# A two-layer encoder kernel on one core: PSUM tiles read by one engine after the other, a negated maximum, scaled memory keys and one copy per Fourier block

## The chip, the core and the metric

The kernel runs on one core of a Trainium2 chip. TensorE (PE in the profile, its weight loads PEld) multiplies, VectorE (DVE) and ScalarE (ACT) read its results from PSUM and prepare the next operands, GpSimd (POOL) does elementwise work between SBUF tiles, and DMA queues, most of them issued by SyncE (SP), bring data from HBM. Each engine works through its own instructions in a fixed order and waits where another engine has not delivered yet. The metric is the device time of one execution in microseconds (us); lower is better.

## What is computed

The reference is an encoder of two layers on 1024 tokens of width 1024, in float32. Cut to what matters:

```python
for l in range(2):
    h = rmsnorm(x, g_pre_mix[l])
    zf, zq, zk, zv, zm = split(h @ w_in[l])          # 256, 512, 128, 128, 256 columns
    y_f = real(fftn(zf, over tokens and channels)) @ w_fourier[l]
    y_a = window_attention(rope(zq), rope(zk), zv, sink[l])      # 8 query heads, 2 key heads, +-128 tokens
    km, vm = split(rmsnorm(mem, g_mem[l]) @ w_mem_kv[l])         # 256 memory rows, 4 heads of 64
    scores = zm @ km.T * 64 ** -0.5
    y_m = softmax(scores) @ vm
    y = concat(rmsnorm(y_f), rmsnorm(y_a), rmsnorm(y_m)) @ w_out[l]
    x = x + rmsnorm(y, g_post_mix[l])
    gate, up = split(rmsnorm(x, g_pre_ffn[l]) @ w_ffn_in[l])
    x = x + rmsnorm((silu(gate) * up) @ w_ffn_out[l], g_post_ffn[l])
```

## The kernel before

**Products.** A float32 product is made of three TensorE products in a rounded format: each operand is split in a high part (ScalarE rounds it by a copy) and a low part (VectorE or GpSimd subtracts the high part from the original), and high x high, high x low and low x high are added up in PSUM (`Acc.add`, L185 to L188). So a result that leaves PSUM and is an operand again is read twice: once by ScalarE for the high part and once by VectorE for the low part.

**Stages of a layer.** The first half of a layer mixes tokens, the second half is the feed-forward network. In the mixing half the kernel goes through: the Fourier columns (`zf`, PSUM tile `zT`), then keys, values and memory queries (`kvz`, tile `kvp`) woven with the Fourier units (`fourier_units`, tiles `yfp` and `yfT`), then the queries (`q`, tile `qp`, L187) woven with the eight memory units (`mem_units`: tile `ms`, L900, for scores, `mpT`, L922, for turned probabilities, `mav`, L932, for values), then window attention of one key head (`att_units(0)`: `sc`, L787, `pT`, L824, `av`, L839) woven with output products (`mo`, L187), then attention of the other key head woven with the second output products, the residual and the first products of the feed-forward network. The feed-forward network (`qc`, `qx`, `qy`, `qz`, L1181, then `fo`, L1330) is long rows of 128x512 products.

**What is touched.** Four helpers read a PSUM tile with both engines, in halves of 64 partitions. `q_stack` (L429) is called twice for one tile, once for each half j: ScalarE copies half j (L433), VectorE then subtracts (L434). Its tiles are `zT` (L730, turned memory queries) and `qT` (L767, turned queries). `dup_stack` (L420) does the same with two copies (L424, L425) and two subtractions (L426, L427) per half; its sources are the PSUM tile `kT` (L736, turned keys) and, in `Memory.load`, the memory keys in SBUF. `fourier_tables` splits `abp` (L529 to L533) half by half, and `fold` (L854) adds the two 64-partition parts of `av`. Between two engines that read the same PSUM tile the kernel carries a wait, in the order in which the code is written, so the second half's ScalarE copy stands behind the first half's VectorE subtraction. `mem_scores` (L889) takes the maximum of two 128x256 score blocks (L902), multiplies it by -1/8 on VectorE (L903) and gives it to the exponentials on ScalarE (L906) as their bias. `Memory.keys` copies the keys out of PSUM (L478). `turned` in the Fourier units copies a turned block out of PSUM with two copies (L610), one for each half of the tokens.

**What sets the order.** The code is traced unit by unit, and a list scheduler at build time then chooses each engine's order from the dependencies, the order of the code and its own estimate of durations. So an edit in one helper can move instructions of other units on all engines. PSUM is held in four pools of two banks each (`sc`, `pT`, `av`, `pd`): a tile that is read late keeps its bank from the next tile of its pool. `qT`, `kT`, `av`, `mav` and the small `ssp` share the pool `av`; `zT` of `kvz_turn`, `yfT`, `mpT` and `abp` share `pT`; `ms`, `sc` and `yfp` share `sc`.

## Time and profile before

| What | Value |
|---|---|
| Time, median of 3 runs (lowest, highest) | 2046.52 us (2045.35, 2047.14) |
| The profiled execution's own time | 2045.68 us |
| Its span, first to last instruction | 2043.9 us |
| DVE, ACT, POOL busy | 1499.5, 1047.9, 691.9 us |
| Mixing half of layer 0, about | 50 to 400 us of the span |
| Mixing half of layer 1, about | 1050 to 1400 us |

The profile comes from one execution; 1.8 us of its time lie outside its span, and it is 0.84 us below the median of the runs. The page names an instruction by its line in the kernel, its engine and its operation, with the tile it writes and those it reads. Idle time of an engine is put down to whatever ended it: `PE ms L900 <- ACT flex L425` means that TensorE stood idle until ScalarE's copy of line 425 was done.

### The profile page before, as it was taken

To read this page: it belongs to the slowest core of one execution; us is meant where nothing else is said; L and a number is where in the kernel's file an instruction comes from. 1 tells how busy PE (TensorE), PEld (TensorE's weight loads), DVE (VectorE), ACT (ScalarE), POOL (GpSimd) and SP (SyncE) were. 2 spreads that over 40 slices of the span, in tenths; PEclk is the share of its full clock that TensorE was granted. 3 is DMA by queue.
4 is the path that set the end of the run, shared out by engine and by line. 5 is a ranking of instruction groups with operands and counts; after the bars stand their busy time and mean duration, and the time that the engine had idled before them with its cause. 6 is when DMAs were issued, how large, how long until landed. Compare 5 with 4: busy or idle time off the path is not lost.

```text
span 2043.9 us, 28334 instructions
## 1 busy us (share of the span) xinstructions
PE 1990.0 (97%) x9587; PEld 1630.4 (80%) x9587; DVE 1499.5 (73%) x2378; ACT 1047.9 (51%) x2220; POOL 691.9 (34%) x811
## 2 busy tenths in 40 slices
PE   7999999999999999999999999999999999999998
PEld 6877777778888888887878768777788888887886
DVE  5566767897867766777956667578887777778776
ACT  7476767643333434554545667676333333346441
POOL 4354445224434332002523544451333433410011
PEclk8999999999999999999999999999999999999999
DMA  6111223433333225979731113243343323269883
GB/s 221 53 57 40 95 99 114 145 129 108 107 110 119 81 90 161 315 262 319 265 127 50 47 47 114 84 145 105 127 135 109 102 99 108 85 229 345 304 276 120
DMA packets 181889, 288.56 MB, mean 141 GB/s; under 512 B 15560, under 2 KB 81648, under 8 KB 181744
## 3 DMA queue, kind: packets, MB, share of 16 engines
q1 hardware_dynamic: 173680, 267.88, 39.2%
q10 hardware_dynamic: 8064, 18.88, 2.4%
q8 instruction: 75, 1.23, 0.2%
q14 instruction: 70, 0.57, 0.1%
HBM read 220.11 MB, written 66.58 MB: 140 GB/s over the span
## 4 chain that ended last, share of the span: by engine, by line
PE 84%; DVE 5%; DMA 3%; ACT 3%; POOL 2%; issue 2%; SPq 0%; DVEq 0%; POOLq 0%; ACTq 0%
PE fo L1330 17%; PE qy L1181 11%; PE qx L1181 11%; PE qc L1181 11%; PE mo L187 7%; PE qz L1181 6%; PE qp L187 4%; PE kvp L187 4%; PE zT L187 2%; PE sc L787 2%; PE pT L824 2%; PE qa L1181 1%; PE mav L932 1%; PE av L832 1%; PE av L839 1%
## 5 line engine op out<-in xcount | busy, mean ns | idle before, releaser
L1330 PE MATMUL fo<-arena_r 128*128 128x512 f32 x1512 | 357.2, 393 | 7.7 <-ACT arena_r L176 3.8
L1330 PEld LDWEIGHTS fo<-arena_r 128*128 128x128 f32 x1512 | 285.2, 189 | 69.0 <-ACT arena_r L176 4.7
L176 ACT CAST arena_r<-arena_f 128x512 fp32r<-128x512 f32 (+2 forms) x344 | 185.5, 571 | 181.9 <-DMA arena_f<-actd 76.1
L177 DVE TENSOR_TENSOR arena_r<-arena_f,arena_r 128x512 fp32r<-128x512 f32 x262 | 182.7, 729 | 52.5 <-ACT arena_r L176 43.2
L1181 PE MATMUL qc<-arena_r,flex 128*128 128x512 f32 x912 | 220.5, 390 | 0.0
L1171 ACT CAST flex<-arena_f 128x512 fp32r<-128x512 f32 x148 | 91.9, 621 | 225.6 <-PE qy L1181 66.4
L1181 PEld LDWEIGHTS qc<-arena_r,flex 128*128 128x128 f32 x912 | 171.0, 188 | 36.8
L1181 PE MATMUL qy<-arena_r,flex 128*128 128x512 f32 x576 | 139.9, 390 | 0.0
L1171 ACT CAST arena_r<-arena_f 128x512 fp32r<-128x512 f32 x92 | 57.1, 621 | 160.7 <-DVE arena_f L1168 71.1
L1172 DVE TENSOR_TENSOR flex<-arena_f,flex 128x512 fp32r<-128x512 f32 x148 | 112.7, 762 | 27.4 <-ACT flex L1171 27.3
L1215 POOL TENSOR_TENSOR arena_f<-arena_f 128x512 f32<-128x512 f32 x36 | 48.3, 1342 | 231.8 <-ACT arena_f L1186 231.8
L1181 PEld LDWEIGHTS qy<-arena_r,flex 128*128 128x128 f32 x576 | 107.8, 188 | 23.1 <-DVE arena_r L177 0.4
L1181 PE MATMUL qx<-arena_r 128*128 128x512 f32 x360 | 119.3, 389 | 0.0
L1181 PE MATMUL qy<-arena_r 128*128 128x512 f32 x480 | 116.1, 389 | 0.0
L1172 DVE TENSOR_TENSOR arena_r<-arena_f,arena_r 128x512 fp32r<-128x512 f32 x92 | 68.2, 741 | 61.5 <-ACT arena_r L1171 61.2
L1181 PE MATMUL qz<-arena_r,flex 128*128 128x512 f32 x320 | 106.5, 395 | 0.0
L1181 PEld LDWEIGHTS qy<-arena_r 128*128 128x128 f32 x480 | 90.1, 188 | 18.7
L1168 DVE TENSOR_TENSOR arena_f<-arena_f 128x512 f32<-128x512 f32 x90 | 97.3, 1085 | 7.3 <-DMA arena_f<-in_w_ffn_in 5.6
L1222 POOL TENSOR_TENSOR arena_f<-arena_f 128x512 f32<-128x512 f32 x36 | 60.0, 1667 | 124.5 <-DVE arena_f L1221 124.5
L235 POOL TENSOR_SCALAR rrsv<-rss 128x1 f32<-128x1 f32 x32 | 14.8, 463 | 257.3 <-ACT arena_f L350 195.8
L1242 POOL TENSOR_TENSOR arena_f<-arena_f,flex 128x512 f32<-128x512 f32 x32 | 54.4, 1701 | 137.8 <-DVE arena_f L1218 53.8
L177 POOL TENSOR_TENSOR arena_r<-arena_f,arena_r 128x256 fp32r<-128x256 f32 (+2 forms) x82 | 67.6, 829 | 98.1 <-ACT arena_r L176 74.1
(316 smaller groups left out, 4777.0 us busy)
## 6 DMA issues: line engine op xcount, KB each, us to landing
arena_f<-in_w_ffn_out SPq DMA_DIRECT2D x264, 256.0 KB, 4.7
actd<-arena_f SPq DMA_DIRECT2D x154, 256.0 KB, 2.7
arena_f<-actd SPq DMA_DIRECT2D x154, 256.0 KB, 4.6
arena_f<-in_w_ffn_in SPq DMA_DIRECT2D x46, 512.0 KB, 3.8
big<-in_w_ffn_in SPq DMA_DIRECT2D x40, 512.0 KB, 4.5
arena_f<-in_w_in SPq DMA_DIRECT2D x40, 256.0 KB, 2.9
arena_f<-in_x SPq DMA_DIRECT2D x16, 512.0 KB, 4.4
arena_f<-in_w_out SPq DMA_DIRECT2D x32, 256.0 KB, 2.7
```

Source lines behind the costliest of these rows:

```text
L176: nc.scalar.copy(hi, src)
L177: return (lo_eng or nc.vector).tensor_tensor(out=lo, in0=src, in1=f32(hi), op=ALU.subtract)
L187: mm(self.dst, a, b, start=self.i == 0, stop=self.i == self.n - 1)
L787: mm(pt, lhs, self.kst[g][i][:, k0 * P : k1 * P], start=i == 0, stop=i == 1)
L1168: nc.vector.tensor_tensor(out=s, in0=x, in1=y, op=op)
L1171: self.cast = nc.scalar.copy(w[:, 0], s)
L1172: nc.vector.tensor_tensor(out=w[:, 1], in0=s, in1=f32(w[:, 0]), op=ALU.subtract)
L1181: mm(pt, a, b, start=start and n == 0, stop=n == 11, skip_group_check=not start)
L1215: G(out=self.u2, in0=self.u2, in1=self.p1, op=ALU.add)
L1222: G(out=self.p5, in0=self.p1, in1=self.p5, op=ALU.add)
L1242: (G if i % 2 else V).tensor_tensor(out=a[i], in0=c, in1=g[i], op=ALU.mult)
L1330: mm(pt, ab[:, 0, x, sl], ab[:, 1, y], start=new and first and j == 0, stop=last and j == 2, skip_group_check=not new)
```

## The change

The reads of a PSUM tile are written engine by engine: `q_stacks` and `dup_stacks` take both halves of a tile, write all ScalarE copies and then all VectorE subtractions; `fourier_tables` and `fold` do the same. `mem_scores` lets the reduction itself negate the maximum and drops the multiplication; the factor 1/8 moves into the copy of the memory keys, and the exponentials lose their scale. `turned` makes one copy of 128x256 in place of two of 128x128. No product is added or taken away: TensorE has the same instructions. Over the whole program VectorE has 32 instructions fewer (the multiplications) and ScalarE 16 fewer (the copies). In the changed kernel the lines are shifted by some numbers: L433 is L435, L610 is L614, L900 is L901, L732 is L736.

```diff
@@ -417,21 +417,25 @@
             acc.add(hsl(hT, half, 0, k, sl), hsl(hT, half, 1, k, sl), w[k][0], w[k][1])
 
 
-    def dup_stack(kh, kl, src, j):
-
-        r = slice(64 * j, 64 * j + 64)
-        o = slice(64 - 64 * j, 128 - 64 * j)
-        nc.scalar.copy(kh[r], src[r])
-        nc.scalar.copy(kh[o], src[r])
-        nc.vector.tensor_tensor(out=kl[r], in0=src[r], in1=f32(kh[r]), op=ALU.subtract)
-        nc.vector.tensor_tensor(out=kl[o], in0=src[r], in1=f32(kh[r]), op=ALU.subtract)
-
-    def q_stack(dst, src, j):
-
-        r = slice(64 * j, 64 * j + 64)
-        o = slice(64 - 64 * j, 128 - 64 * j)
-        nc.scalar.copy(dst[r], src[r])
-        nc.vector.tensor_tensor(out=dst[o], in0=src[r], in1=f32(dst[r]), op=ALU.subtract)
+    def dup_stacks(dsts, src):
+
+        for j, (kh, kl) in enumerate(dsts):
+            r, o = slice(64 * j, 64 * j + 64), slice(64 - 64 * j, 128 - 64 * j)
+            nc.scalar.copy(kh[r], src[r])
+            nc.scalar.copy(kh[o], src[r])
+        for j, (kh, kl) in enumerate(dsts):
+            r, o = slice(64 * j, 64 * j + 64), slice(64 - 64 * j, 128 - 64 * j)
+            nc.vector.tensor_tensor(out=kl[r], in0=src[r], in1=f32(kh[r]), op=ALU.subtract)
+            nc.vector.tensor_tensor(out=kl[o], in0=src[r], in1=f32(kh[r]), op=ALU.subtract)
+
+    def q_stacks(dsts, src):
+
+        for j, dst in enumerate(dsts):
+            r = slice(64 * j, 64 * j + 64)
+            nc.scalar.copy(dst[r], src[r])
+        for j, dst in enumerate(dsts):
+            r, o = slice(64 * j, 64 * j + 64), slice(64 - 64 * j, 128 - 64 * j)
+            nc.vector.tensor_tensor(out=dst[o], in0=src[r], in1=f32(dst[r]), op=ALU.subtract)
 
 
     class Memory:
@@ -475,7 +479,7 @@
             acc = Acc(pt, NK)
             for k in range(NK):
                 acc.add(self.wk[ci][k][0], self.wk[ci][k][1], self.m(0, k), self.m(1, k))
-            nc.scalar.copy(at(self.ks + ci, NMEM), pt)
+            nc.scalar.activation(at(self.ks + ci, NMEM), pt, AF.Copy, scale=QK_SCALE)
 
         def values(self, mt):
             pt = ps([MW], "vmp", self.tag)
@@ -505,8 +509,7 @@
             km = shaped(reflex(F32R), (2, 2, 2, NMEM))
             self.km = [km[:, i] for i in range(2)]
             for ci in range(2):
-                for j in range(2):
-                    dup_stack(self.km[ci][:, j, 0], self.km[ci][:, j, 1], raw[:, ci], j)
+                dup_stacks([(self.km[ci][:, j, 0], self.km[ci][:, j, 1]) for j in range(2)], raw[:, ci])
 
 
     class Mix:
@@ -528,9 +531,11 @@
                 for s in range(2):
                     pt = ps([HD], "abp", "pT")
                     mm(pt, cc[:, s, :], wf, start=True, stop=True)
-                    for j in range(2):
-                        r = slice(64 * j, 64 * j + 64)
-                        split(AB[r, pr, 0, s, j, :], AB[r, pr, 1, s, j, :], pt[r])
+                    rs = [slice(64 * j, 64 * j + 64) for j in range(2)]
+                    for j, r in enumerate(rs):
+                        nc.scalar.copy(AB[r, pr, 0, s, j, :], pt[r])
+                    for j, r in enumerate(rs):
+                        nc.vector.tensor_tensor(out=AB[r, pr, 1, s, j, :], in0=pt[r], in1=f32(AB[r, pr, 0, s, j, :]), op=ALU.subtract)
             self.AB = AB
             self.PQ = {}
 
@@ -586,7 +591,7 @@
                 TT(E[0], A[0], A[1], ALU.add)
                 TT(E[1], A[0], A[1], ALU.subtract)
                 yf = at(48, 2, 2, 512)
-                self.yf = [yf[:, i] for i in range(2)]
+                self.yf, self.yfs = [yf[:, i] for i in range(2)], yf
 
             def products(r):
                 th, tl, dh, dl = st.pop(("d", r))
@@ -606,11 +611,10 @@
                 pT = ps([2, P], "yfT", "pT")
                 for i in range(2):
                     nc.tensor.transpose(pT[:, i, :], y[:, i * P : (i + 1) * P], ident)
-                for half in range(2):
-                    nc.scalar.copy(
-                        self.yf[half].rearrange("p k (c r) -> p k c r", r=8)[:, :, :, r],
-                        pT[:, :, half * 64 : half * 64 + 64],
-                    )
+                nc.scalar.copy(
+                    self.yfs.rearrange("p h k (c r) -> p h k c r", r=8)[:, :, :, :, r],
+                    pT.rearrange("p k (h c) -> p h k c", h=2),
+                )
 
             def halves(r, dst):
                 raw = raws(2, P)
@@ -730,16 +734,14 @@
             zt = ps([2, P], "zT", "pT")
             for pr in range(2):
                 nc.tensor.transpose(zt[:, pr, :], z[:, pr * P : pr * P + P], ident)
-            for j in range(2):
-                q_stack(self.zst[half][j][:, :, c * P : c * P + P], zt, j)
+            q_stacks([self.zst[half][j][:, :, c * P : c * P + P] for j in range(2)], zt)
             if c == 0:
                 self.kt = ps([4, P], "kT", "av")
             nc.tensor.transpose(self.kt[:, c, :], kr.rearrange("p h d -> p (h d)"), ident)
             if c == 3:
                 ktf = self.kt.rearrange("p c t -> p (c t)")
                 sl = slice(half * 512, half * 512 + 512)
-                for g in range(2):
-                    dup_stack(self.kst[g][0][:, sl], self.kst[g][1][:, sl], ktf, g)
+                dup_stacks([(self.kst[g][0][:, sl], self.kst[g][1][:, sl]) for g in range(2)], ktf)
 
         def skewed(self, f, g, n):
 
@@ -769,8 +771,7 @@
                 nc.tensor.transpose(qt[:, pr, :], qr[:, pr * P : pr * P + P], ident)
             if c == 0:
                 self.qst[half] = [at((64, 0)[half] + 8 * i, 4, 512, dt=F32R) for i in range(2)]
-            for j in range(2):
-                q_stack(self.qst[half][j][:, :, c * P : c * P + P], qt, j)
+            q_stacks([self.qst[half][j][:, :, c * P : c * P + P] for j in range(2)], qt)
 
 
         def att_scores(self, g, n):
@@ -855,10 +856,11 @@
 
             cut = lambda ap: ap.rearrange("p (h s q) -> p s h q", s=2, q=P)
             avh, avl = cut(av[0:64]), cut(av[64:128])
+            d = [dst[64 * s : 64 * s + 64] for s in range(2)]
             for s in range(2):
-                d = dst[64 * s : 64 * s + 64]
-                nc.scalar.copy(d, avl[:, s])
-                nc.vector.tensor_tensor(out=d, in0=avh[:, s], in1=d, op=ALU.add)
+                nc.scalar.copy(d[s], avl[:, s])
+            for s in range(2):
+                nc.vector.tensor_tensor(out=d[s], in0=avh[:, s], in1=d[s], op=ALU.add)
 
         def att_units(self, g):
 
@@ -888,7 +890,6 @@
 
         def mem_scores(self, h, half):
             e = [ems(2, NMEM) for _ in range(2)]
-            rmax = sm(4, "rmax")
             nmx = sm(4, "nmx")
             den = sm(4, "den")
             for b in range(2):
@@ -899,12 +900,11 @@
                     for i in range(2):
                         mm(pt[:, j], lhs, self.mem.km[h // 2][:, h % 2, i], start=i == 0, stop=i == 1)
                 bs = slice(2 * b, 2 * b + 2)
-                nc.vector.tensor_reduce(out=rmax[:, bs], in_=pt, axis=AX.X, op=ALU.max)
-                nc.vector.tensor_scalar_mul(nmx[:, bs], rmax[:, bs], -QK_SCALE)
+                nc.vector.tensor_reduce(out=nmx[:, bs], in_=pt, axis=AX.X, op=ALU.max, negate=True)
                 for j in range(2):
                     c = 2 * b + j
                     nc.scalar.activation(
-                        e[b][:, j], pt[:, j], AF.Exp, bias=nmx[:, c : c + 1], scale=QK_SCALE, accum_out=den[:, c : c + 1]
+                        e[b][:, j], pt[:, j], AF.Exp, bias=nmx[:, c : c + 1], accum_out=den[:, c : c + 1]
                     )
             rden = sm(4, "rden")
             nc.vector.reciprocal(rden, den)
```

The scheduler makes a new order of all engines in the mixing halves; in the long rows of the feed-forward network hardly anything moves. Three places follow, without the numbers of the rows.

The first place is ScalarE at the end of the key stage of layer 0, where the last turned keys (`kT`) and memory queries (`zT`) are stacked; what each instruction waits for stands in brackets. Before:

```order
L424 CAST arena_r<-kT_1168 64x512 [waits PE_49]
L425 CAST arena_r<-kT_1168 64x512
L424 CAST arena_r<-kT_1168 64x512 [waits DVE_49]
L425 CAST arena_r<-kT_1168 64x512
L610 COPY arena_f<-yfT_1371 128x128 [waits PE_49]
L610 COPY arena_f<-yfT_1371 128x128
L433 CAST flex_92<-zT_1376 64x2x128 [waits PE_49]
```

After:

```order
L424 CAST arena_r<-kT_1165 64x512 [waits PE_49]
L425 CAST arena_r<-kT_1165 64x512
L424 CAST arena_r<-kT_1165 64x512
L425 CAST arena_r<-kT_1165 64x512
L614 COPY arena_f<-yfT_1365 128x256 [waits PE_49]
L435 CAST flex_92<-zT_1369 64x2x128 [waits PE_49]
L435 CAST flex_92<-zT_1369 64x2x128
```

The third copy of `kT` no longer waits for VectorE, each Fourier block has one copy, and both copies of `zT` stand in a row; before, the second one stood eight copies of the memory keys later.

TensorE at the same place goes from the first query products (`qp`) to the first memory scores (`ms`). Before:

```order
L187 MATMUL qp_1397<-big_1349,arena_r 128x512 x2
L187 MATMUL qp_1493<-big_1349,arena_r 128x512 x2
L900 MATMUL ms_1466<-flex_1437,arena_r 128x256
L900 MATMUL ms_1475<-flex_1437,arena_r 128x256
L900 MATMUL ms_1466<-flex_1437,arena_r 128x256 x3
L900 MATMUL ms_1475<-flex_1437,arena_r 128x256 x3
```

After:

```order
L187 MATMUL qp_1389<-big_1343,arena_r 128x512 x2
L187 MATMUL qp_1479<-big_1343,arena_r 128x512 x2
L901 MATMUL ms_1454<-flex_1429,arena_r 128x256
L901 MATMUL ms_1462<-flex_1429,arena_r 128x256
L187 MATMUL qp_1556<-big_1319,arena_r 128x512 x6
L187 MATMUL qp_1556<-big_1327,arena_r 128x512 x6
L187 MATMUL qp_1556<-big_1335,arena_r 128x512 x6
L187 MATMUL qp_1556<-big_1343,arena_r 128x512 x3
L901 MATMUL ms_1454<-flex_1429,arena_r 128x256 x3
L901 MATMUL ms_1462<-flex_1429,arena_r 128x256 x3
```

The first two score products need the high part of the memory keys, the third needs the low part; 21 query products now stand between them.

The second place is TensorE at the start of the query products of layer 1. `big_9724` and `big_9732` (`big_9686` and `big_9694` after) hold the weights of the first and second, and of the third and fourth, 128 input rows; of each row block three products are made. Before:

```order
L187 MATMUL qp_9796<-big_9724,arena_r 128x512 x3
L732 MATMUL zT_9625<-const,arena_f 128x128 x2
L187 MATMUL qp_9796<-big_9724,arena_r 128x512 x3
L187 MATMUL qp_9796<-big_9732,arena_r 128x512 x6
L187 MATMUL qp_9796<-big_9740,arena_r 128x512 x3
L608 MATMUL yfT_9654<-const,flex_2276 128x128 x2
L732 MATMUL zT_9690<-const,arena_f 128x128 x2
L187 MATMUL yfp_9705<-arena_r 128x256 x6
```

After:

```order
L187 MATMUL qp_9756<-big_9686,arena_r 128x512 x5
L736 MATMUL zT_9589<-const,arena_f 128x128 x2
L187 MATMUL qp_9756<-big_9694,arena_r 128x512 x3
L187 MATMUL qp_9831<-big_9686,arena_r 128x512 x6
L187 MATMUL qp_9831<-big_9694,arena_r 128x512 x3
L740 MATMUL kT_9532<-const,arena_f 128x128
L187 MATMUL qp_9756<-big_9694,arena_r 128x512
L187 MATMUL qp_9831<-big_9694,arena_r 128x512
L613 MATMUL yfT_9618<-const,flex_2244 128x128 x2
L736 MATMUL zT_9653<-const,arena_f 128x128 x2
L187 MATMUL yfp_9668<-arena_r 128x256 x6
L187 MATMUL qp_9756<-big_9694,arena_r 128x512 x2
```

One product of `qp_9756` more has moved ahead of these rows. The low part of the fourth row block is first needed by the 11th query product before, and by the 21st after; a second token tile (`qp_9831`), six Fourier products and four transposes now stand ahead of it.

The third place is TensorE at the end of the query products of layer 1. Before:

```order
L187 MATMUL qp_10366<-big_9748,arena_r 128x512 x2
L187 MATMUL qp_10366<-big_9748,flex_4658 128x512
L932 MATMUL mav_10268<-arena_f 64x512 x3
L900 MATMUL ms_10244<-flex_9830,flex_4102 128x256 x4
L900 MATMUL ms_10253<-flex_9830,flex_4102 128x256 x4
```

After:

```order
L187 MATMUL qp_10305<-big_9702,flex_4626 128x512
L901 MATMUL ms_10271<-flex_9790,flex_4070 128x256 x4
L187 MATMUL qp_10305<-big_9710,arena_r 128x512 x2
L187 MATMUL qp_10305<-big_9710,flex_4626 128x512
L901 MATMUL ms_10279<-flex_9790,flex_4070 128x256 x4
```

`ms_10244` and `ms_10253` are the scores of the sixth of the eight memory units, and they follow the last query product; `ms_10271` and `ms_10279` are those of the seventh, and they stand ahead of it. Three units came behind the query products before, and one does after.

## Prediction

> **What bounds the kernel now.** I read the page first: busy times and the shares of the chain of work that ended last.
>
> ```profile
> PE 1990.0 (97%) x9587; PEld 1630.4 (80%) x9587; DVE 1499.5 (73%) x2378; ACT 1047.9 (51%) x2220; POOL 691.9 (34%) x811
> PE 84%; DVE 5%; DMA 3%; ACT 3%; POOL 2%; issue 2%; SPq 0%; DVEq 0%; POOLq 0%; ACTq 0%
> ```
>
> TensorE is busy for 1990.0 of 2043.9 us, so 53.9 us of idle time is all that a change of waits can win, and the change leaves its instructions alone. DVE and ACT can lose work without any gain, unless TensorE waits for them. So the second view is the waits of TensorE, then the waits that the change is about, on ACT:
>
> ```profile
> PE qp L187 <- POOL big L177: 2.8, 1, 2.8
> PE hTp L1106 <- DVE arena_f L321: 2.3, 1, 2.3
> PE ms L900 <- ACT flex L425: 2.2, 1, 2.2
> PE ms L900 <- DVE flex L427: 0.9, 1, 0.9
> ```
>
> ```profile
> ACT arena_f L906 <- DVE nmx L903: 13.3, 9, 4.3
> ACT arena_r L433 <- DVE arena_r L434: 11.1, 11, 3.4
> ```
>
> ACT loses 11.1 us to the handoff that the change takes away, and 13.3 us to the multiplication of the maximum. But both are ACT's idle time, not TensorE's. TensorE is directly held by copies of this kind in one place, the memory scores: 2.2 us for L425 and 0.9 us for L427. The third view is the windows, to see how much idle time lies in the stretches whose order changes, and at which clock:
>
> ```profile
> core 0: us, PE busy (x) PEld busy (x) DVE busy (x) ACT busy (x) POOL busy (x), PEclk, DMA share, GB/s
> 136.00:145.00 9.00, 6.16 (x29) 5.12 (x30) 8.78 (x16) 6.39 (x16) 4.52 (x6) 1.00 0.01 3
> 200.00:213.00 13.00, 11.61 (x64) 7.21 (x62) 9.56 (x33) 10.21 (x33) 5.71 (x13) 1.00 0.18 62
> 1130.00:1140.00 10.00, 7.17 (x30) 5.77 (x29) 6.08 (x9) 7.40 (x20) 7.01 (x10) 0.83 0.31 103
> 1195.00:1218.00 23.00, 19.72 (x101) 11.87 (x99) 20.31 (x42) 18.56 (x51) 10.98 (x18) 1.00 0.30 92
> 1360.00:1400.00 40.00, 35.59 (x198) 27.42 (x198) 32.30 (x47) 27.42 (x59) 18.10 (x30) 0.97 0.54 174
> 1500.00:1600.00 100.00, 100.00 (x440) 82.36 (x439) 75.48 (x85) 35.52 (x62) 40.35 (x26) 1.00 0.33 110
> ```
>
> First column after the window is its length, then TensorE's busy time. Idle: 2.84 us where the memory scores of layer 0 start (136 to 145), 1.39 at the end of its query products (200 to 213), 2.83 at the start of those of layer 1 (1130 to 1140, clock 0.83), 3.28 at their end (1195 to 1218), 4.41 around the entry of a feed-forward network, none in its middle. So the whole stake is some 10 to 12 us, half a per cent.
>
> **The change part by part.** *Row order in the query, key and memory-query stacks.* One copy and one subtraction of a turned query tile:
>
> ```profile
> L433 ACT CAST arena_r<-qT x32: 569/582/594, 149.3 to 1211.1; 64x512 fp32r<-64x512 f32 x32
> L434 DVE TENSOR_TENSOR arena_r<-qT,arena_r x32: 674/688/694, 149.9 to 1212.5; 64x512 fp32r<-64x512 f32 x32
> ```
>
> Before, a tile goes copy, subtraction, copy, subtraction in one chain: 2 x (0.58 + 0.69) = 2.5 us. After, the second copy runs beside the first subtraction: 0.58 + 2 x 0.69 = 1.96 us when nothing else stands between, so 0.6 us less per tile. The first consumers of most tiles stand many products later, and there this costs or wins nothing. The exception is the key tile of layer 0:
>
> ```profile
> 134.04 0.68 DVE L427 TENSOR_TENSOR arena_r<-kT,arena_r 64x512 fp32r<-64x512 f32 x1
> 134.76 0.58 ACT L424 CAST arena_r<-kT 64x512 fp32r<-64x512 f32 x1 [1.45 <-DVE arena_r L427]
> ...
> 136.37 0.41 ACT L433 CAST flex<-zT 64x256 fp32r<-64x256 f32 x1
> ...
> 137.98 0.50 PE L900 MATMUL ms<-flex,arena_r 128*128 128x256 f32 x2 [2.19 <-ACT flex L425]
> ...
> 139.35 0.98 PE L900 MATMUL ms<-flex,arena_r 128*128 128x256 f32 x6 [0.86 <-DVE flex L427]
> ```
>
> Columns: start, duration, engine, line, operation; in brackets the idle time before it and what ended it. ACT stood idle for 1.45 us at 134.76 because of the handoff, and TensorE for 2.19 us at 137.98 because ACT's next copies (of the memory keys, L425) came late. Of the 2.19 I take 1.45 - 0.41 = 1.04 off, 0.41 being the second copy of `zT` that now stands ahead of the key copies. The second wait, 0.86, is for the low part of the memory keys; 21 query products now stand ahead of it, each
>
> ```profile
> 491.76 2.73 PE qx L1181 x12
> ```
>
> 2.73 / 12 = 0.2275 us, 4.8 us in all, over five times 0.86. The wait goes whole. **Term 1: 1.04 + 0.86 = 1.9 us**, bounds 0 (the copies come late all the same, and the products that now stand between are missed later) and 3.05 (both waits whole).
>
> *The start of the query products of layer 1.*
>
> ```profile
> 1129.15 1.87 PE L187 MATMUL qp<-big,arena_r 128*128 128x512 f32 x7
> ...
> 1132.10 1.69 POOL L177 TENSOR_TENSOR big<-arena_f,big 128x512 fp32r<-128x512 f32 x1
> ...
> 1133.85 2.05 PE L187 MATMUL qp<-big,arena_r 128*128 128x512 f32 x5 [2.83 <-POOL big L177]
> ...
> 1135.13 1.26 POOL L177 TENSOR_TENSOR big<-arena_f,big 128x512 fp32r<-128x512 f32 x1
> ...
> 1140.01 1.29 POOL L177 TENSOR_TENSOR big<-arena_f,big 128x512 fp32r<-128x512 f32 x1 [0.25 <-ACT big L176]
> 1141.05 0.88 PE L187 MATMUL yfp<-arena_r 128*128 128x256 f32 x6
> ```
>
> TensorE waits 2.83 us for the low part of the fourth weight block, ready at 1132.10 + 1.69 = 1133.79. The five products behind it take 2.05 / 5 = 0.41 us each, against 0.2275: the clock fell, and the window's 0.83 puts that at 0.17 x 10 = 1.7 us. At most 2.83 + 1.7 = 4.5 us can go. In the changed order ten more query products (2.3 us) and six Fourier products (0.9 us by the last row) stand ahead of the first use of that block: 3.2 us, enough to cover 2.83. What is late next is the following low parts, ready at 1136.39 and 1141.30; their times are set by loads and by GpSimd, which the change leaves alone, and TensorE would reach them earlier by what it has gained. So part comes back. **Term 2: 1.4 us**, half of 2.83, bounds -1 (the wait comes back longer, by about one wait as at 139.35) and 4.5.
>
> The Trainium skill, page "TensorE: Matmul & The Clock Gate", section "HAM oscillation — how this bites in real kernels", gives as the rule that TensorE should not idle for more than about 3.4 us at once, or its clock is halved; the 2.83 us at 1133.85 were shorter and the clock fell all the same, so this trace does not bear out that figure. By the page the 1.7 us would not hang on this wait, the upper bound of the term would be 2.83, and the best total 2035.9.
>
> *Negated maximum and scaled keys.* The way from a score block to its exponentials, around 202 us:
>
> ```profile
> 201.08 0.69 DVE L902 TENSOR_REDUCE rmax<-ms 128x2 f32<-128x512 f32 x1
> 201.80 0.77 DVE L974 SCALAR_TENSOR_TENSOR big<-arena_f,const,big 128x512 fp32r<-128x512 f32 x1
> 202.49 0.16 DVE L903 TENSOR_SCALAR nmx<-rmax 128x2 f32<-128x2 f32 x1
> 203.46 0.49 ACT L906 ACTIVATE arena_f<-ms,nmx 128x256 f32<-128x256 f32 x1
> ```
>
> The reduction ends at 201.77, the exponential starts at 203.46: 1.69 us, in which the multiplication and a foreign operation of 0.77 us that VectorE had put in between both go. The multiplications themselves:
>
> ```profile
> L903 DVE TENSOR_SCALAR nmx<-rmax x32: 155/169/1041, 146.7 to 1214.3; 128x2 f32<-128x2 f32 x32
> L610 ACT COPY arena_f<-yfT x32: 371/436/515, 100.2 to 1147.7; 128x128 f32<-128x128 f32 x32
> ```
>
> 32 x 0.17 = 5.4 us of VectorE's work, all of it beside TensorE's: 0 as work. Whether a negating reduction costs more than 0.69 no row shows; I take the same, as it reads the same 512 columns, with 0.17 more at the worst, which is the operation it replaces. A scaled copy of the keys for a plain one I take at equal price too; it lies in the loading of the memory, long before its use. What counts is that a unit's chain is shorter and that the scheduler places the units earlier: one memory unit stands behind the last query product of layer 1 and not three, so two units' chains of waits get query products as cover. At the two ends of the query products 1.39 and 3.28 us are idle. VectorE is busy there for 20.31 of 23 us, so it can itself stay the one waited for: I take half. **Term 3 (layer 1): 1.6 us**, bounds 0 and 3.28. **Term 4 (layer 0): 0.7 us**, bounds 0 and 1.39.
>
> *One copy per Fourier block, the fold, the `abp` split.* A 128x256 copy costs between 0.44 and 2 x 0.44 us in place of two of 0.44, so up to 16 x 0.44 = 7 us of ACT's work goes. It lies in the stage of keys and the start of the queries, where ACT is busy 7.40 of 10 us and TensorE does not wait for `yfT` copies in the list. 0. The fold and `abp` copies likewise: 0, covered by attention products and by the start of the layer.
>
> *Sum.* 1.9 + 1.4 + 1.6 + 0.7 = 5.6 us. 2045.68 - 5.6 = 2040.1 for an execution like the profiled one; the profiled one was 0.84 below the median, so **2040.9**. With all upper bounds, 3.05 + 4.5 + 3.28 + 1.39 = 12.2: 2034.3. With all lower ones, -1: 2047.5.
>
> **The rivals.** Changes under 0.2%, 4.1 us, can hardly be told from none here: faster is below 2042.4, slower above 2050.6.
>
> *Waits that move (same).* TensorE stays the bound, and what it gains at layer 1 it loses at the next load or low part: VectorE is busy 20.31 of 23 us at the end of the queries. Only Term 1 stays: 2045.68 - 1.9 + 0.84 = 2044.6. For it: no row shows a direct wait of TensorE for L433 or L434. Against it: the units do move.
>
> *Everything goes (faster).* All upper bounds, 2034.3. For it: the moved products cover each wait by length. Against it: weights still come from loads.
>
> *A new wait at the entry of the feed-forward network (slower).* The new order in the mixing half shifts the residual and norm work on VectorE against TensorE's first feed-forward products. There is one such wait already:
>
> ```profile
> 1395.82 0.66 PE L1106 MATMUL hTp<-const,arena_f 128*128 128x128 f32 x4 [2.27 <-DVE arena_f L321]
> ```
>
> One more like it with the loss of clock seen above, 2.27 + 1.7 = 4.0 us in each layer, is 8.0; less Term 1 that is 2045.68 + 8.0 - 1.9 + 0.84 = 2052.6. It decides when new waits exceed the gains by over 4.1 us. Against it: VectorE has less work, not more, and the rows of the feed-forward network hardly move.
>
> *The row order does nothing (same).* If the two halves of a tile could be read by both engines at once without a wait, the row order would remove nothing, and only Terms 3 and 4 would be left: 2045.68 - 2.3 + 0.84 = 2044.2. Against it stands the 1.45 us at 134.76, a wait of this very kind. The Trainium skill, page "PSUM — Partial Sum Buffer", section "PSUM bank collisions raise a hardware error", says that two engines may use one bank at once in different groups of 32 partitions, and the halves here are 64 partitions each; by that page the wait is not needed, but the trace shows that the kernel carries it.
>
> **How the numbers follow.** Forecast 0.48, its own range 2038 to 2043, so 0.40 of it faster and 0.08 same; moved waits 0.25 and no effect of the row order 0.03, same; everything goes 0.12, faster; the new wait 0.12, slower. Faster 0.52, same 0.36, slower 0.12. The range takes in the bounds, 2034.3 and 2047.5, and a little more on each side for the run; it leaves out the slower rival: 2034 to 2048.5.
>
> **What would show it.** In the profile after: the third `kT` copy with no wait for VectorE, and no wait of `ms` for the low part of the memory keys near 138 us (Term 1); a granted clock of 1.00 and no idle over 1.4 us in the first ten us of layer 1's queries (Term 2); idle time at the ends of the query products halved (Terms 3 and 4); no exponential that waits 1.69 us behind its reduction. I am wrong if TensorE's idle time is the same with other names on it, if the waits at the entry of the feed-forward network grow over 4 us, or if the negating reduction takes visibly over 0.69 us.

## The result and the profile after

The changed kernel takes 2032.75 us (median of 6 runs, 2029.83 to 2034.12) beside 2045.93 us for the kernel before on the same chip; the ratio is 0.9944, 95% interval 0.9928 to 0.9960. The absolute median lies 1.25 us below the range of the prediction; 0.9944 of the 2046.52 us shown is 2035.1, inside it. The gain is 13.2 us by the medians and 11.5 by the ratio, over twice the forecast 5.6. The busy times and the chain of waits, from the page of the changed kernel:

```profile
PE 1984.7 (98%) x9587; PEld 1631.2 (80%) x9587; DVE 1492.6 (74%) x2346; ACT 1049.7 (52%) x2204; POOL 684.9 (34%) x811
PE 86%; DVE 5%; DMA 3%; ACT 2%; issue 2%; POOL 1%; SPq 0%; DVEq 0%; POOLq 0%; ACTq 0%
```

VectorE lost 6.9 us of work and ScalarE gained 1.8, so the single copies did not show as less work of ScalarE, though one takes 0.664 us where two took 0.87. The span is 2030.4 us against 2043.9. The windows that answer to the five of before, moved by what each place has moved:

```profile
core 0: us, PE busy (x) PEld busy (x) DVE busy (x) ACT busy (x) POOL busy (x), PEclk, DMA share, GB/s
138.00:147.00 9.00, 6.90 (x23) 5.15 (x22) 8.82 (x13) 4.20 (x11) 3.69 (x5) 0.81 0.04 16
200.00:213.00 13.00, 12.21 (x69) 8.32 (x65) 11.19 (x30) 11.14 (x29) 3.89 (x7) 1.00 0.33 110
1132.00:1142.00 10.00, 8.27 (x43) 6.56 (x42) 7.70 (x14) 8.09 (x21) 6.60 (x11) 1.00 0.27 85
1193.00:1216.00 23.00, 22.38 (x118) 15.06 (x116) 17.22 (x48) 20.07 (x57) 9.54 (x17) 1.00 0.37 125
1347.00:1387.00 40.00, 38.55 (x214) 29.74 (x213) 33.40 (x51) 28.75 (x66) 21.83 (x29) 1.00 0.54 171
```

TensorE's idle time (length less busy) goes from 2.84 to 2.10 us at the first memory scores, from 1.39 to 0.79 at the end of layer 0's query products, from 2.83 to 1.73 at the start of layer 1's and from 3.28 to 0.62 at their end. The clock moved too: 0.83 became 1.00 at the start of layer 1's queries, 1.00 became 0.81 at the first memory scores. There, in order of time:

```profile
139.88 0.38 PE L901 MATMUL ms<-flex,arena_r 128*128 128x256 f32 x1 [1.27 <-ACT flex L425]
...
141.09 0.36 PE L901 MATMUL ms<-flex,arena_r 128*128 128x256 f32 x1 [0.83 <-DVE flex L438]
141.29 6.58 PE L187 MATMUL qp<-big,arena_r 128*128 128x512 f32 x21
```

The first wait fell from 2.19 to 1.27. The wait for the keys' low part is gone behind the 21 query products, but the second score product now waits 0.83 us for VectorE's subtraction of `zT` (L438), and those 21 products take 6.58 us instead of 21 x 0.2275 = 4.78.

To see where the 13.5 us lie I take the first TensorE instruction of a stage as its start; a mixing half starts with its first `kvp` product. Differences from the first profile of the kernel before, in us:

| kernel | start | layer 0 mixing | FFN | FFN output | layer 1 mixing | FFN | FFN output |
|---|---|---|---|---|---|---|---|
| changed kernel | +2.8 | -2.0 | -0.5 | -5.4 | -8.7 | +0.2 | +0.1 |
| changed kernel, second profile (e7) | +2.1 | -2.1 | -0.5 | -5.9 | -8.2 | +0.3 | -3.2 |
| kernel before, second profile (e0) | -0.5 | +3.7 | 0.0 | -5.8 | -0.6 | -0.2 | +0.5 |

The third row is the same program as the one subtracted, so it shows what chance does: 3.7 us in one stage and 5.8 in another. The 5.4 us at the output of layer 0's feed-forward network are therefore not the change's. Of the two mixing columns only layer 1's is beyond that by itself. Together they are 10.7 and 10.3 us less than the first profile of before, 13.9 and 13.4 less than the second. The 3.7 us go with the clock: by the clock records of the traces, layer 0's mixing half lost 5.1 us to a lower clock in e0, nothing in the first profile of before, and 3.4 in the changed kernel, which hides part of its gain there. TensorE's share of the two halves, as the sum of their two windows, before (64.52 to 381.22 and 1044.18 to 1390.57) and after (67.31 to 381.97 and 1039.09 to 1376.79):

```profile
sum 663.09, PE 646.14 PEld 519.13 DVE 457.05 ACT 450.85 POOL 303.50; mean PE 323.07 PEld 259.57 DVE 228.52 ACT 225.42 POOL 151.75
```

```profile
sum 652.36, PE 642.21 PEld 521.02 DVE 453.38 ACT 453.34 POOL 301.64; mean PE 321.10 PEld 260.51 DVE 226.69 ACT 226.67 POOL 150.82
```

TensorE's idle time falls from 663.09 - 646.14 = 16.95 to 652.36 - 642.21 = 10.15 us: 6.8 of the 10.7 us are waits that went. The other 3.9 us lie in time that the trace counts as busy, and no row here says where.

### The profile page after: what moved, and what is told of

It is laid out like the page before. It is cut to its first block, busy times and chain, and to the rows that moved or that the text cites. A ratio compares the mean times of both kernels' runs of the same rounds, so it can differ in the third digit from the quotient of the medians.

```text
span 2030.4 us, 28325 instructions
## 1 busy us (share of the span) xinstructions
PE 1984.7 (98%) x9587; PEld 1631.2 (80%) x9587; DVE 1492.6 (74%) x2346; ACT 1049.7 (52%) x2204; POOL 684.9 (34%) x811
## 4 chain that ended last, share of the span: by engine, by line
PE 86%; DVE 5%; DMA 3%; ACT 2%; issue 2%; POOL 1%; SPq 0%; DVEq 0%; POOLq 0%; ACTq 0%
PE fo L1330 17%; PE qc L1181 11%; PE qx L1181 11%; PE qy L1181 11%; PE mo L187 8%; PE qz L1181 5%; PE kvp L187 4%; PE qp L187 3%; PE zT L187 2%; PE sc L788 2%; PE pT L825 2%; PE av L833 1%; PE qa L1181 1%; PE mav L932 1%; PE av L840 1%
## 5 line engine op out<-in xcount | busy, mean ns | idle before, releaser
L187 PE MATMUL mo<-big,arena_r 128*128 128x512 f32 x384 | 100.2, 399 | 0.3 <-ACT arena_f L1031 0.2
L1181 PE MATMUL qx<-flex,flex 128*128 128x512 f32 x304 | 100.1, 390 | 0.0
```

The costliest lines, as they stand in the source:

```text
L187: mm(self.dst, a, b, start=self.i == 0, stop=self.i == self.n - 1)
L1181: mm(pt, a, b, start=start and n == 0, stop=n == 11, skip_group_check=not start)
```

## The experiments

Two theories stood after the result. One: each part takes away the waits that it is about, and the gain is their sum. Two: the list scheduler makes a new order from the changed code, and the order is the gain. The ratios below are to the kernel before on the same chip; its medians there were 2043.81 us for e0 to e3, 2043.62 for e4 to e7 and 2044.45 for e8 to e11.

### The kernel before again (e0)

> The kernel before once more, unchanged, for a second profile of it. Of the 13.5 us between the two profiled spans, about 5.9 lie at the end of layer 0, where TensorE of the kernel before waited 1.16 and 1.45 us for operands loaded back from HBM (1030.91 and 1032.86 us) and then ran 12 products at half pace. Theory (the waits belong to the kernel's order): the second profile shows the same two waits of TensorE there, and the ratio is 1.000. Rival (a load that landed late by chance in one execution): no wait there over 0.5 us, and the second profiled span is 2036 to 2040 us with the rest of the trace alike.

Measured: 2040.60 us, ratio 0.9982 (0.9967 to 0.9996). An unchanged copy comes out 0.18% faster, and its interval leaves out 1: differences of 0.2% and a little more are not settled by such runs. The only wait of TensorE from 999 to 1046 us in its timeline, and then the two of the first profile:

```profile
1008.73 0.66 PE L341 MATMUL hTp<-const,arena_f 128*128 128x128 f32 x4 [1.11 <-DVE arena_r L177]
```

```profile
1030.91 0.49 PE L1330 MATMUL fo<-arena_r 128*128 128x512 f32 x1 [1.16 <-ACT arena_r L176]
1032.86 5.49 PE L1330 MATMUL fo<-arena_r 128*128 128x512 f32 x12 [1.45 <-DVE arena_r L177]
```

The rival holds here: the two waits belong to one execution (the profiled span of e0, 2041.0 us, is 1 us above what the rival gave). The medians carry no such single event, but the runs scatter: 2037.8 to 2052.5 us over 29 of one program.

### One part at a time (e1, e2, e3), and two of them (e6)

e1 takes the row order alone (`dup_stacks`, `q_stacks`, the `abp` split and the fold as in the change), e3 the single Fourier copy alone. e2, in which the exponentials lose their scale too:

```diff
-            nc.scalar.copy(at(self.ks + ci, NMEM), pt)
+            nc.scalar.activation(at(self.ks + ci, NMEM), pt, AF.Copy, scale=QK_SCALE)
...
-                nc.vector.tensor_reduce(out=rmax[:, bs], in_=pt, axis=AX.X, op=ALU.max)
-                nc.vector.tensor_scalar_mul(nmx[:, bs], rmax[:, bs], -QK_SCALE)
+                nc.vector.tensor_reduce(out=nmx[:, bs], in_=pt, axis=AX.X, op=ALU.max, negate=True)
```

> Only the row order (all ScalarE copies of a tile, then VectorE), in the stacks, the abp split and the fold; the multiplication of the maximum and the two Fourier copies stay. Theory (each part saves the waits it is about): 1.0 us at the first memory scores of layer 0 and 1 to 3 us in layer 1, ratio 0.998 to 0.999. Rival (the list scheduler's new order decides, and the parts are not worth anything by themselves): the ratio lies anywhere between 0.995 and 1.002, and the TensorE waits that differ are not at tiles with the new row order.

> Only the negated maximum and the scaled memory keys. Theory: the ends of the query products gain, 0.6 us in layer 0 and 2.7 us in layer 1 by the two traces, ratio 0.998 to 0.9985. Rival (order by chance): between 0.995 and 1.002, with the idle time at the ends of the query products of 1.4 and 3.3 us as before.

> Only one copy of 128x256 in place of two of 128x128 per Fourier block, 16 ScalarE copies fewer. Theory: ScalarE's work there is beside TensorE's, 0, ratio 0.9995 to 1.0005. Rival (order by chance): off 1 by 0.1% or more to either side.

> Negated maximum, scaled keys and one copy per Fourier block; the row order of the kernel before. If the parts add up: 0.9936 x 0.9972 = 0.991. If each part only makes another order and the orders do not add: 0.993 to 0.997.

Measured: row order 0.9993 (0.9978 to 1.0008), maximum 0.9936 (0.9918 to 0.9955), single copy 0.9972 (0.9958 to 0.9987), maximum and copy together 0.9933 (0.9910 to 0.9957). The negated maximum alone gives all that the whole change gives, and over three times what theory one gave it; it lies below the range of its rival too. Nothing adds to it. The single copy's ratio overlaps that of the unchanged copy, so it stays open whether it is worth anything. The orders of e1, e2 and e6 brought something along. From e2's timeline, in the first feed-forward network:

```profile
439.68 0.73 PE L1179 MATMUL qy<-arena_r,flex 128*128 128x512 f32 x2 [2.31 <-ACT flex L1169]
```

All three carry this wait, and behind it either a second wait of 1.7 us or as much of lost clock (the rows are in the last section). That stage is 4.1 us longer in each; in e3 and the changed kernel the wait is not there.

### Code and order apart (e4, e5)

Here code and order are parted. Each kernel lists the instructions of every engine by number and ties each to the one ahead of it, without a semaphore:

```diff
+    for order in _ORDER.values():
+        ins = [traced[f"I-{n}"] for n in order if f"I-{n}" in traced]
+        for a, b in zip(ins, ins[1:]):
+            tc.add_manual_dep(b, a.name, info, reason="order")
```

e4 is e2's code in the order of the kernel before, e5 the code of before in e2's order.

> The code of e2_max_only (negated maximum, scaled keys), but with every engine's instructions tied to the order that they have in the kernel before; only the 32 multiplications are missing from VectorE's row. Theory (the gain is the new order that the list scheduler makes out of the shorter chain): nearly nothing is left of it, ratio 0.998 to 1.000, and the end of layer 1's query products still idles about 3.3 us. Rival (the gain is the shorter chain itself, 0.17 us and one handoff less per unit): most of it is there, ratio 0.9935 to 0.996.

> The code of the kernel before, multiplications and unscaled keys included, but with every engine's instructions tied to the order that they have in e2_max_only (the multiplications, which that kernel lacks, are placed by the scheduler). Theory (order): most of the gain, ratio 0.994 to 0.997. Rival (chain): 0.998 to 1.002, since each unit's chain is as long as before.

Measured: e4 0.9990 (0.9975 to 1.0005), e5 1.0003 (0.9988 to 1.0018). Neither code nor order does it alone, so both theories fall as they were put; the two together make 0.9936. TensorE's longest waits in layer 1 from the query products to the feed-forward network: the kernel before (its two longest, 2.8 and 2.3 us, stand in the prediction), then e4, e5 and e2:

```profile
PE mpT L922 <- POOL arena_f L912: 1.9, 3, 0.8
```

```profile
PE qp L187 <- POOL big L177: 2.8, 1, 2.8
PE hTp L1104 <- DVE arena_f L321: 2.3, 1, 2.3
PE mpT L920 <- POOL arena_f L910: 2.0, 3, 1.0
```

```profile
PE qp L187 <- POOL big L177: 2.2, 1, 2.2
PE mpT L922 <- POOL arena_f L912: 1.5, 1, 1.5
PE av L839 <- DVE arena_r L177: 0.8, 1, 0.8
```

```profile
PE qp L187 <- POOL big L177: 2.0, 1, 2.0
PE av L839 <- DVE arena_r L177: 0.8, 1, 0.8
```

e4 has the waits of the kernel before, one for one, though 32 multiplications are missing. All waits listed there add up to 12.2 us before, 11.6 in e4, 6.6 in e5 and 4.2 in e2: the order takes away some 6 of the 8 us, and with the multiplication put back `mpT` waits again. In the total e5 has nothing of it, because the 4.1 us of the first feed-forward network come with e2's order (4.2 in e5) and layer 0's mixing is 3.1 us longer than in e2.

Why it needs both can be read from one score block. e4, then e2: VectorE's reduction, and the first exponential of that block:

```profile
205.22 0.69 DVE L901 TENSOR_REDUCE nmx<-ms 128x2 f32<-128x512 f32 x1 [0.31 <-PE ms L899]
207.70 0.47 ACT L904 ACTIVATE arena_f<-ms,nmx 128x256 f32<-128x256 f32 x1
```

```profile
189.27 0.68 DVE L901 TENSOR_REDUCE nmx<-ms 128x2 f32<-128x512 f32 x1
190.37 0.48 ACT L904 ACTIVATE arena_f<-ms,nmx 128x256 f32<-128x256 f32 x1
```

From the reduction's end to the exponential's start: 207.70 - 205.91 = 1.79 us in e4, 190.37 - 189.95 = 0.42 in e2. Worked out so for all 32 blocks from the timelines, the median is 1.54 us in the kernel before, 1.33 in e4, 1.39 in e5, 0.12 in e2 and 0.26 in the changed kernel. In e4 the exponentials still stand behind other work on ScalarE. In e5 they stand early, but the multiplication does not follow its reduction at once: it starts 0.76 us behind it in the median. A chain of three instructions through two queues is short only when every queue has its place for it.

### The changed kernel again (e7), and its code and order apart (e8 to e11)

> The changed kernel once more, beside the three above on one chip, for a second profile of it. If the first measurement stands: 0.993 to 0.996. If it owed part to a kernel before that was slow in its runs by chance (its unchanged copy came out at 0.998): 0.995 to 0.998. In the profile the waits of the mixing half of layer 1 are those of the first profile to 0.3 us, and the stretch from 1000 us to the first kvp product is within 1 us of it.

> The code of e1_rows_only with every engine's instructions tied to the order of the kernel before, so only the waits between ScalarE and VectorE on one PSUM tile change. Theory (waits gone and order new pay only together): 0.999 to 1.001; in the profile ScalarE's wait of 1.45 us before its third kT copy is gone and TensorE's wait at the first memory scores of layer 0 falls from 2.2 us to 1.0 to 1.3. Rival (the row order pays by itself): 0.996 to 0.998.

> All edits of the changed kernel, every engine's instructions tied to the order of the kernel before. Theory: 0.998 to 1.000, TensorE's waits in layer 1 (2.8, 2.3, 2.0 and 1.5 us) stay to 0.3 us. Rival (edits pay by themselves): 0.993 to 0.996, as the changed kernel.

> The code of the kernel before with every engine's instructions tied to the order of the changed kernel; the 32 multiplications and the 16 second copies that have no place in it are put in by the scheduler. The order of e2_max_only under the old code gave 1.000, but it carries 4.1 us more in the first feed-forward network, which the changed kernel's order does not. Theory (the order carries about two thirds of the mixing half's gain, the shorter chains the rest): 0.996 to 0.998. Rival (an order pays only with the code it was made for): 0.999 to 1.002.

> The changed kernel with the multiplication of the maximum and the unscaled keys put back, in the order of the changed kernel. Set beside e10 it tells what row order and single copy add in this order, beside the changed kernel what the negated maximum adds. Theory (the memory units' chain is what the order was made short for): as e10, 0.996 to 0.998. Rival (the row order is): 0.993 to 0.996, as the changed kernel.

Measured: e7 2030.78 us, 0.9941 (0.9922 to 0.9960), so the first measurement stands. Of the two signs in its profile neither held quite: TensorE's wait for `kT` in layer 1 is 0.8 us instead of 0.3, and the first `kvp` product stands 1.25 us earlier. e8 1.0190 (1.0169 to 1.0212) and e9 1.0170 (1.0143 to 1.0196): slower by 1.7 to 1.9%, which no theory had. e10 1.0105 (1.0085 to 1.0125), also slower. e11 0.9986 (0.9972 to 1.0000).

e8 was to lose ScalarE's wait for VectorE. The 1.45 us before the third `kT` copy are gone, but TensorE's first memory scores wait 1.70 and 4.32 us. VectorE's waits in the kernel before, then in e8, then two of TensorE's in e8:

```profile
DVE arena_r L434 <- ACT arena_r L433: 12.9, 19, 3.1
DVE flex L861 <- ACT flex L860: 2.8, 4, 1.9
```

```profile
DVE arena_r L438 <- ACT arena_r L435: 35.3, 18, 5.5
DVE flex L864 <- ACT flex L862: 20.6, 12, 3.1
```

```profile
PE av L841 <- DVE arena_r L177: 7.7, 6, 3.7
PE ms L903 <- DVE flex L429: 4.8, 2, 4.3
```

In this order the row order turns the wait round: VectorE's first subtraction now stands behind ScalarE's second copy. Where that copy comes late, VectorE, the busier of the two, holds back what TensorE needs, and each mixing half gets some 21 us longer (by the stages as in the table: +20.7 and +21.7). In the order that the scheduler makes for it, the second copy is moved up: in e1 ScalarE's 11.1 us of waiting for L434 are gone and VectorE's wait for the copies is 14.2 us instead of 12.9. Still the total neither loses nor wins (0.9993), as ScalarE's idle time was not TensorE's. e10 is e8 the other way round; two of ScalarE's waits there, 11.1 and 2.4 us in the kernel before:

```profile
ACT arena_r L433 <- DVE arena_r L434: 35.2, 24, 4.6
...
ACT flex L860 <- DVE flex L861: 22.6, 16, 3.0
```

e11 is the changed kernel with only the multiplication and the unscaled keys back, in the changed kernel's order. In its list of waits (the same two are 26.7 and 0.3 us in the changed kernel):

```profile
ACT arena_f L908 <- DVE nmx L905: 33.6, 14, 6.0
...
PE sc L788 <- ACT arena_f L908: 2.6, 2, 2.1
```

A ratio of 0.9986 against 0.9941 and 0.9944: the negated maximum is worth about 9 us in that order by the ratios, 7.3 by the stages (the mixing halves of e11 are 3.0 us below the first profile of before, those of e7 10.3). e11 is as good as the kernel before or 0.1% better, which is all that row order and single copy can claim against it. In the order made for them they are worth more beside e10, the old code in that order: 1.0105 against 0.9986. An order can cost with code that it was not made for.

## Why the prediction came out as it did

The sign was right, and so was one of the two mechanisms: the memory units' shorter chain, placed earlier, takes waits of TensorE away in the mixing halves, and engine work as such gives nothing. The other mechanism, the row order, gives nothing in the total by itself. The size was too small, 5.6 us against 11.5 to 13.2, and that the ratio's 2035.1 us still lies inside the range is partly luck: the range went down to 2034 by upper bounds of the four terms, Term 1's of 3.05 among them, and not by the places where the rest was won. Of the signs named, the third `kT` copy has lost its wait for VectorE and the clock at the start of layer 1's queries is 1.00, but there is a wait of 1.73 us there, not 1.4 at most, and four of 32 exponential blocks still start more than 1.69 us behind their reduction (13 before).

- **Term 1, 1.9 us for the row order at the first memory scores.** The first wait fell by 0.92 (1.04 forecast). The 0.86 did not go: a wait of 0.83 on another subtraction took its place, and with the clock at 0.81 (0.19 x 9 = 1.7 us) the place lost about 0.7 us by these waits; the clock there is chance, as the last section shows. The step that failed is the source of the term: the row order by itself gives 0.9993, and in the order of the kernel before it costs 1.9%. I had counted ScalarE's wait of 1.45 us that goes and not VectorE's that comes. In the changed kernel the first subtraction of `kT` stands behind all four copies and starts 1.2 us after the second one's end (136.07 us); before, it started at once:

```profile
137.28 0.68 DVE L428 TENSOR_TENSOR arena_r<-kT,arena_r 64x512 fp32r<-64x512 f32 x1 [4.04 <-ACT arena_r L425]
```

- **Term 2, 1.4 us at the start of layer 1's queries.** Idle time 1.1 less and 1.7 of clock: 2.8, twice the term and inside its bounds. The wait of 2.83 us for GpSimd's low part is gone, and one of 1.73 for VectorE's low part (L407) came. This term does come from the row order's schedule: e1 has 1.66 us there at a clock of 1.00, e2 has 2.02 and loses clock. But in e1 layer 1's mixing half is only 0.5 us shorter; the rest is lost again elsewhere in it. (With 2.83 as the upper bound of this term the best total would be 2036.0, not 2035.9.)
- **Term 3, 1.6 us, and Term 4, 0.7.** 2.66 and 0.60. The half that I took for the end of layer 1's query products was too small: the waits there were mostly for the scaled probabilities (`mpT`), at the end of the memory units' chain, and not for VectorE's other work. They stay in e4, where that chain is late, and go in e2, where it is not.
- **Multiplications and keys at 0 as work.** Right: e4 is 0.9990 without them. The negating reduction takes 0.690 us in the median against 0.691, the scaled key copy 0.383 against 0.373. But I sized what the shorter chain is worth by the idle time at two places, 2.3 us in all. It is worth 7 to 9 us, and what stands behind the memory units gains as well. The windows of layer 1's attention, before and after, have 172.00 - 169.11 = 2.89 and 169.00 - 167.92 = 1.08 us of idle time:

```profile
1218.00:1390.00 172.00, 169.11 (x951) 136.20 (x950) 122.20 (x306) 127.68 (x330) 83.56 (x136) 1.00 0.32 110
```

```profile
1207.00:1376.00 169.00, 167.92 (x945) 135.05 (x946) 124.03 (x312) 130.02 (x336) 82.45 (x135) 1.00 0.35 118
```

- **The rivals.** The new wait in the feed-forward network was real, at about the price that I gave one such wait (4.1 us against 4.0): it sits in layer 0 of e1, e2, e5 and e6, by chance of the order not in the changed kernel. In layer 1 the changed kernel trades the 2.27 us at the entry for 2.3 of `qy` later, in sum 0.2 us. That the row order is worth nothing came out in the number (e1), but not by the rival's mechanism: the two halves of a tile do carry waits, as e8 shows. The absolute time came closest to the rival in which all waits go, but they did not all go; the terms make 2.8 + 2.66 + 0.60 - 0.7 = 5.4 us against 5.6 forecast, which is near by chance, as Term 1's loss and the gain of the others cancel. Of the rest of the mixing halves' 10.7, layer 1's attention has 1.8 of idle time; where the other 3.5 come from the rows do not show. I had put all of that at nothing.

What stays open: whether the single copy is worth 0.1%, and how much of the 0.6% is a lucky order. That another order can cost 4.1 us in one place is shown by e2. No run ties the kernel before to its own order; that the ties themselves cost nothing rests on e4, whose total and waits are those of before. And in e5, e10 and e11 the scheduler placed the multiplications, so on VectorE those orders are not quite the ones they stand for.

## What to carry to other kernels

Where a scheduler orders the queues, an edit pays only through the order made for it: cost its chain by the time from producer's end to consumer's start in the trace (1.54 us here), not by the duration of the instruction that goes (0.17). Writing all reads of one engine ahead of those of the next takes the first engine's wait away and makes the second one stand behind the last of the first: ask which of the two holds up the bound engine, and whether the order lets the first one's reads come early. And run an unchanged copy beside the change before believing a few tenths of a per cent.

## What the runs showed of the hardware

I had not expected that a wait of nearly the same length at the same place costs clock in one execution and not in another. In the two profiles of the kernel before, TensorE waits 2.19 and 2.25 us at the first memory scores. The 8 us from there on, first profile, then e0:

```profile
137.98:145.98 8.00, 7.14 (x34) 5.92 (x35) 7.80 (x14) 4.46 (x9) 4.52 (x6) 1.00 0.01 3
```

```profile
137.59:145.59 8.00, 7.35 (x23) 5.98 (x24) 7.79 (x15) 4.45 (x9) 4.50 (x6) 0.57 0.01 3
```

34 products at a clock of 1.00, 23 at 0.57: 0.43 x 8 = 3.4 us of clock, and e0's mixing half of layer 0 is 3.7 us longer. Behind the 1.27 and 0.83 us of the changed kernel, at the same place, the clock was 0.81. The Trainium skill, page "TensorE: Matmul & The Clock Gate", section "HAM oscillation — how this bites in real kernels", gives idle gaps of more than about 3.4 us as what halves the clock; these rows show it fall behind much shorter ones, not each time. No single wait need be long: in e3 the clock is 0.50 from 281.94 to 285.35 us, and in the ten us ahead no wait of TensorE is over 0.22 us.

Lost clock is not always lost time. Behind the 2.31 us wait of `qy`, in layer 0 of e2 and of e5, the windows and the next wait read:

```profile
439.68:447.68 8.00, 8.00 (x35) 6.50 (x36) 8.00 (x9) 2.19 (x4) 5.13 (x3) 1.00 0.38 129
```

```profile
452.62 0.73 PE L1179 MATMUL qx<-arena_r,flex 128*128 128x512 f32 x2 [1.70 <-DVE flex L1170]
```

```profile
444.40:452.40 8.00, 7.99 (x28) 6.47 (x29) 8.00 (x9) 2.11 (x4) 5.12 (x3) 0.79 0.40 130
```

```profile
457.38 0.73 PE L1181 MATMUL qx<-arena_r,flex 128*128 128x512 f32 x2 [0.17 <-DVE flex L1172]
```

e2 runs 35 products in the 8 us, e5 28, which is 0.21 x 8 = 1.7 us of clock. But e2 then waits 1.70 us for VectorE and e5 0.17: from the end of the one wait to the end of the other it is 452.62 - 439.68 = 12.94 us in e2 and 457.38 - 444.41 = 12.97 in e5, and the stage is 4.1 and 4.2 us longer. TensorE was early or slow; VectorE set the time. Over whole runs clock and time do go together: of 29 runs of the kernel before, the eight with a mean clock of 0.990 or less took 2047.7 us in the mean, the six with 0.994 or more 2041.5. What the rest of the 15 us is, loads from HBM as at 1030 us for instance, is not shown.
